# A diffusion trunk in float32: the last FFN's gated units as seven half-size products instead of eight

## The chip, the cores and the metric

The kernel runs on one core of a Trainium2 chip. The metric is the time of the whole program on the device in microseconds (us); the median of three runs is 1763.65 us (1762.95 to 1763.93). Engines are named as the profile names them: PE is TensorE's matmul, PEld its weight load, DVE VectorE, ACT ScalarE, POOL GpSimd, SP SyncE, which issues the loads.

## The reference

Two layers work on 512 latent and 256 context tokens of width 1024: latent attention in layer 0, a state-space layer (S5) with a gated output (GLU) in layer 1, and after each a gated FFN with 2816 hidden units. Each sub-layer begins with an RMSNorm and a modulation (scale and shift computed from a conditioning vector) and ends with a gated residual. Only latent tokens leave layer 1. What the change touches is the second layer's FFN:

```python
def modulate(x, g, shift, scale):
    return rmsnorm(x, g) * (1 + scale) + shift

def swiglu(h, w_in, w_out):
    a, b = jnp.split(h @ w_in, 2, axis=-1)
    return (jax.nn.silu(a) * b) @ w_out

xl = xl + gt2_l * swiglu(modulate(xl, norm_ffn[i], sh2_l, sc2_l), ffn_w_in[i], ffn_w_out[i])
```

## The kernel before

Everything is held transposed: 128 channels on the partitions, tokens along the columns. x has eight such rows of channels (KT = 8). Every float32 product is done as three products of a rounded type: an operand is split into a high part (a copy on ScalarE, rounded) and a low part (the difference, on VectorE; `split`, L74 to L81), and `passes` (L812 to L818) adds high x high, high x low and low x high in PSUM. So a linear layer with eight rows of channels takes 24 matmuls for each 128 outputs, each of them with its own weight load.

The FFN has 22 hidden tiles of 128 units. A *gated unit* is one of them: two weight tiles of 128x1024 (for a and b), two PSUM accumulators of 512 columns, 48 matmuls, then silu(a) on ScalarE (L873), the product with b on VectorE (L874) and the split of the result u. `BLOCKS` (L827) cuts layer 1's 22 units into blocks of 8, 7 and 7. After each block follow eight *output tiles*: the block's u's times `ffn_w_out` (24 or 21 matmuls of 512 columns), added to x on VectorE with the gate (`residual`, L801). After the last block each row of x is stored by SP (L890).

Weights come through one stream (`Stream`, `load`, `halve`, L83 to L125): a specification names the next weight; `take` loads up to two ahead (four, while an extra pool is open) and has one more split ahead. Raw weights, high and low parts have two buffers each (tags w_raw, w_hi, w_lo). `ada_rows` (L243 to L276) computes the rest of the modulation terms on VectorE: for each of eight rows a 128x1024 product with accumulation, two rows a step, pinned to the order of the program (`keep_in_program_order`); in layer 1's FFN they are stepped once a unit. The rest of the order on each engine is chosen by the scheduler when the program is built, which takes, of what it holds ready, the earliest in the program.

Layer 1's FFN comes right behind the GLU, which is done in two halves of 256 tokens (`HALVES`): products of 256 columns, sigmoid, residual, and the sum of squares for the norm. Each half ends with `modulate` (L346 to L356), which makes the FFN's input hh, hl for that half. `first1` computes the first two gated units half by half, so that TensorE works on the first half while the second half's norm is made.

Of the kernel before, what the change touches and what calls it, by code (L numbers as in the profile page):

```python
# [10 lines left out]
F32 = mybir.dt.float32  # L11
F32R = mybir.dt.float32r
AF = mybir.ActivationFunctionType
# [36 lines left out]
def trunk_kernel(ctx: ExitStack, tc: tile.TileContext, ins: dict, outs: dict):  # L50
# [5 lines left out]
    def pool(name, **kw):  # L56
        return tc.tile_pool(name=name, bufs=1, reuse_waits="tile", **kw)
# [242 lines left out]
    def mod(layer, term):  # L300
        return mods[layer][:, 8 * term : 8 * term + 8, :]
# [524 lines left out]

    BLOCKS = ([(0, 5), (5, 10), (10, 14), (14, 18), (18, 22)], [(0, 8), (8, 15), (15, 22)])  # L827

    def ffn_specs(layer):
        for bi, (b0, b1) in enumerate(BLOCKS[layer]):  # L830
            for ht in range(b0, b1):
                for j in range(2):
                    yield ins["ffn_w_in"][layer, ht, j], KT * P, f"wi{layer}_{ht}_{j}", layer * j > 0
            for m in range(KT):
                yield (ins["ffn_w_out"][layer, m, :, b0:b1, :].rearrange("p a b -> p (a b)"), (b1 - b0) * P,
                       f"wo{layer}_{bi}_{m}", layer * m % 2 > 0)

    def specs():
        for p_ in range(2):
            for m in range(KT):  # L840
                yield ins["mla_w_o"][m], KT * P, f"wmo{p_}_{m}", m % 2 == 0 and p_ + m > 0
        yield from ffn_specs(0)
# [5 lines left out]
        yield from ffn_specs(1)  # L848

    stream.specs = iter(specs())  # L850

    def ffn(layer, parts, pf, first, ops, hooks, norm=None, ahead=None):
        blocks = BLOCKS[layer]
        n = parts[-1][2]
        ub = max(b - a for a, b in blocks)
        gate = mod(layer, 5)
        for bi, (b0, b1) in enumerate(blocks):
            uh = pf.tile([P, ub, n], F32R, tag="uh", name=f"uh{layer}_{bi}")
            ul = pf.tile([P, ub, n], F32R, tag="ul", name=f"ul{layer}_{bi}")
            uops = [(part_of(uh, p_), part_of(ul, p_)) for p_ in parts]  # L860
            for ht in range(b0, b1):
                if ht == 0:
                    firsts = first()
                if ht < len(firsts):
                    ab = firsts[ht]
                else:
                    ab = accs_for(parts, f"f{layer}_{ht}", 2)
                    for acc in ab:
                        linear(acc, stream.take(), ops)
                sa = pf.tile([P, n], F32, tag="sa", name=f"sa{layer}_{ht}", bufs=1)  # L870
                u = pf.tile([P, n], F32, tag="u", name=f"u{layer}_{ht}", bufs=1 + layer)
                for acc, accb, (_, a, b) in zip(*ab, parts):
                    nc.scalar.activation(sa[:, a:b], acc, AF.Silu)  # L873
                    nc.vector.tensor_mul(u[:, a:b], accb, sa[:, a:b])  # L874
                split(uh[:, ht - b0, :], ul[:, ht - b0, :], u)
                next(hooks, None)
            for m in range(KT):
                w = stream.take()
                acc, = accs_for(parts, f"fo{layer}_{bi}_{m}")
                linear(acc, w, uops, b1 - b0)  # L880
                for z, p_ in zip(acc, parts):
                    residual(z, p_, m, gate)
                if m in EXTRA:
                    next(hooks, None)
                if norm is not None and b1 == HT:
                    norm.add(m, x[:, m, :])
                    if m == 3:
                        ahead()
                if layer and b1 == HT:
                    nc.sync.dma_start(outs["out"][:, m, :], x[:, m, :NL])  # L890

    def begin(ab, ws, i, ops, ks=range(KT)):

# [4 lines left out]
    with pool("pd") as pd:  # L898
# [48 lines left out]
        with pool("pf0") as pf:  # L947
# [71 lines left out]
            sp, mix = {}, {}  # L1019
            it = hooks0()  # L1020
            norm = Norm(pd, T, "2")
            ffn(0, PARTS, pf, first, ops, it, norm, ahead)
        chunk_roots(norm)


    with pool("pg") as pg:
# [36 lines left out]
        with pool("ph", side="right") as ph, ExitStack() as wx:  # L1063
            more["pool"] = wx.enter_context(pool("wx1"))
            hh = ph.tile([P, KT, NL], F32R, tag="hh", name="hh_f1")
            hl = ph.tile([P, KT, NL], F32R, tag="hl", name="hl_f1")
            tiles = [lambda nm, n: ph.tile([P, n], F32, tag="hm", name=nm, bufs=4)]
            for p_ in HALVES:
                _, a, b = p_
                norm = Norm(ph, b - a, f"3_{a}")  # L1070
                for m in range(KT):
                    if m == 0:
                        ab = [[acc[0][:, a:b]] for acc in both]
                    else:
                        ab = accs_for([p_], f"gl{a}_{m}", 2)
                        for acc in ab:
                            linear(acc, stream.take(), [gated(a, b)])
                    sg = ph.tile([P, b - a], F32, tag="sg", name=f"sg{a}_{m}", bufs=2)
                    nc.scalar.activation(sg, ab[1][0], AF.Sigmoid)
                    z = ph.tile([P, b - a], F32, tag="z", name=f"gz{a}_{m}", bufs=2)  # L1080
                    nc.vector.scalar_tensor_tensor(z, ab[0][0], mod(1, 2)[:, m, 0:1], sg, op0=ALU.mult, op1=ALU.mult)
                    nc.vector.tensor_add(x[:, m, a:b], x[:, m, a:b], z)
                    norm.add(m, x[:, m, a:b])
                modulate(p_, 3, mod(1, 3), part_of(hh, p_), part_of(hl, p_), norm.bcast(), tiles)
# [10 lines left out]
            with pool("pf1") as pf:  # L1095
                ffn(1, [(0, 0, NL)], pf, first1, [(hh, hl)], ada_rows(pf, 40, 48, 2))
    banks.close()


def s5_prep(nc, const, pp, ps1, ins, ident, dsk, i16, sp):  # L1100
# [564 lines left out]
```

## Time and profile before

| | us |
|---|---|
| median of three runs | 1763.65 |
| the profiled execution, own time | 1765.18 |
| its span on the core | 1763.4 |
| busy in it: PE / DVE / ACT / POOL | 1646.2 / 1077.5 / 690.8 / 590.0 |
| last FFN in it, from the end of the GLU (1397) to the end | 366 |

A row of the chain or the timeline begins with the time from the span's start in us and the length in us; "x" is the number of instructions merged in the row. A row of a group gives line, engine, operation, what is written and read, shapes and count, then busy us, the mean of one in ns, and the idle time of the engine just before these instructions with what ended it. A row of the table by stage gives the stretch, its length, the busy us of each engine (with its instructions), TensorE's granted clock as a share of full speed, the busy share of the DMA engines, and GB/s.

### The profile page before, as it was taken

The numbers are of one execution on the slowest core, as the hardware profiler recorded it, in microseconds if no ns is written. First come the engines' busy times: TensorE is split into PE (matmuls) and PEld (weight loads), VectorE is DVE, ScalarE is ACT, GpSimd is POOL, SyncE is SP. The second block draws the span as 40 slices with busy tenths as digits, with TensorE's granted clock in tenths as the row PEclk, the third lists the DMA queues.
The fourth block names the chain that finished last, engine by engine and source line by source line (L and its number), as shares of the span: only waits on it lengthen the run. The fifth ranks groups of instructions, "written<-read, shape, count | busy, mean of one in ns | idle before, by whom it ended". The sixth has DMA issues, their size and how long they took to land. (4 is left out here: it accounts for less than half of the span.)

```text
span 1763.4 us, 29083 instructions
## 1 busy us (share of the span) xinstructions
PE 1646.2 (93%) x11486; PEld 1406.3 (80%) x11486; DVE 1077.5 (61%) x1881; ACT 690.8 (39%) x1400; POOL 590.0 (33%) x626
## 2 busy tenths in 40 slices
PE   6979999999999999999989989976799999999999
PEld 5868878777888887877778878865579988888887
DVE  5787868787997356575566434547965654333332
ACT  3447757677453212222222312246525543232221
POOL 0156454510235247586667300046741100000000
PEclk9999989999999999999999999988879999999999
DMA  9130001124424355566435554353536452333231
GB/s 337 42 119 15 15 12 30 57 81 152 163 85 141 111 176 155 162 195 185 137 117 176 172 203 147 123 180 132 197 123 199 147 175 88 108 91 100 96 88 68
DMA packets 79832, 224.76 MB, mean 127 GB/s; under 512 B 8912, under 2 KB 24144, under 8 KB 77520
## 3 DMA queue, kind: packets, MB, share of 16 engines
q1 hardware_dynamic: 77472, 219.67, 38.4%
q10 hardware_dynamic: 2224, 3.24, 0.5%
q8 instruction: 90, 1.47, 0.3%
q14 instruction: 46, 0.38, 0.1%
HBM read 192.53 MB, written 30.34 MB: 126 GB/s over the span
## 5 line engine op out<-in xcount | busy, mean ns | idle before, releaser
L77 ACT ACTIVATE wh_wi<-wr_wi 128x1024 fp32r<-128x1024 f32 x88 | 93.2, 1061 | 321.6 <-PE f L818 259.5
L80 DVE TENSOR_TENSOR wl_wi<-wr_wi,wh_wi 128x1024 fp32r<-128x1024 f32 x88 | 116.3, 1323 | 130.4 <-ACT wh_wi L77 129.4
L818 PE MATMUL f<-hhh,wl_wi 128*128 128x512 f32 (+1 forms) x704 | 185.5, 341 | 5.0 <-DVE wl_wi L80 5.0
L818 PE MATMUL f<-hhl,wh_wi 128*128 128x512 f32 (+1 forms) x704 | 184.5, 340 | 0.0
L818 PE MATMUL f<-hhh,wh_wi 128*128 128x512 f32 (+1 forms) x704 | 183.7, 340 | 0.1
L818 PE MATMUL fo<-uh,wl_wo 128*128 128x512 f32 (+1 forms) x528 | 161.3, 361 | 9.0 <-DVE wl_wo L80 9.0
L818 PE MATMUL fo<-uh,wh_wo 128*128 128x512 f32 (+1 forms) x528 | 162.7, 364 | 4.3 <-ACT wh_wo L77 2.6
L818 PE MATMUL fo<-ul,wh_wo 128*128 128x512 f32 (+1 forms) x528 | 162.4, 361 | 3.4 <-DVE ul L80 3.4
L326 POOL TENSOR_TENSOR sqa<-sqa,sq 128x256 f32<-128x256 f32 (+2 forms) x25 | 37.9, 1515 | 323.3 <-ACT sq L324 321.5
L77 ACT ACTIVATE wh_wo<-wr_wo 128x512 fp32r<-128x512 f32 (+3 forms) x64 | 50.5, 793 | 239.9 <-PE fo L818 112.7
L818 PE MATMUL f<-hl_f,wh_wi 128*128 128x512 f32 (+1 forms) x384 | 142.8, 372 | 0.0
L818 PE MATMUL f<-hh_f,wl_wi 128*128 128x512 f32 (+1 forms) x384 | 142.6, 372 | 0.0
L818 PE MATMUL f<-hh_f,wh_wi 128*128 128x512 f32 (+1 forms) x384 | 142.1, 372 | 0.0
L801 DVE SCALAR_TENSOR_TENSOR x<-fo,mods,x 128x512 f32<-128x512 f32 x104 | 63.4, 644 | 120.4 <-PE fo L818 120.4
L818 PEld LDWEIGHTS f<-hhh,wl_wi 128*128 128x128 f32 x704 | 109.8, 190 | 21.0 <-DVE wl_wi L80 5.9
L818 PEld LDWEIGHTS f<-hhh,wh_wi 128*128 128x128 f32 x704 | 109.0, 189 | 17.1 <-issue 1.0
L818 PEld LDWEIGHTS f<-hhl,wh_wi 128*128 128x128 f32 x704 | 109.0, 189 | 15.7 <-issue 0.6
L818 PEld LDWEIGHTS fo<-uh,wl_wo 128*128 128x128 f32 x528 | 88.9, 192 | 24.0 <-DVE wl_wo L80 10.0
L818 PEld LDWEIGHTS fo<-uh,wh_wo 128*128 128x128 f32 x528 | 89.3, 193 | 19.7 <-ACT wh_wo L77 3.1
L818 PEld LDWEIGHTS fo<-ul,wh_wo 128*128 128x128 f32 x528 | 89.6, 193 | 18.6 <-DVE ul L80 4.3
L80 DVE TENSOR_TENSOR wl_wo<-wr_wo,wh_wo 128x512 fp32r<-128x512 f32 (+3 forms) x64 | 60.4, 947 | 55.1 <-ACT wh_wo L77 54.9
L709 ACT ACTIVATE pth<-pt 128x384 fp32r<-128x384 f32 (+1 forms) x160 | 71.8, 470 | 42.1 <-PE pt L705 40.7
(401 smaller groups left out, 4033.0 us busy)
## 6 DMA issues: line engine op xcount, KB each, us to landing
wr_wi<-ffn_w_in SPq DMA_DIRECT2D x88, 512.0 KB, 3.7
adaw<-ada_w SPq DMA_DIRECT2D x72, 512.0 KB, 4.5
wr_wg<-s_w_glu SPq DMA_DIRECT2D x30, 512.0 KB, 3.5
adat<-ada_t SPq DMA_DIRECT2D x24, 512.0 KB, 4.9
wr_wmo<-mla_w_o SPq DMA_DIRECT2D x16, 512.0 KB, 3.6
s_wout<-v SPq DMA_DIRECT2D x64, 128.0 KB, 2.6
s_win<-big SPq DMA_DIRECT2D x16, 512.0 KB, 4.8
s5win<-s_win SPq DMA_DIRECT2D x7, 1024.0 KB, 4.8
```

The source lines that it names most:

```text
L77: ins_ = nc.scalar.activation(hi, src, AF.Copy)
L80: eng.tensor_tensor(lo, src, hi.bitcast(F32), ALU.subtract)
L326: nc.gpsimd.tensor_tensor(self.acc, self.acc, sq, ALU.add)
L709: nc.scalar.activation(dh, pt3, AF.Copy)
L801: nc.vector.scalar_tensor_tensor(x[:, m, a:b], acc, gate[:, m, v : v + 1], x[:, m, a:b], op0=ALU.mult, op1=ALU.add)
L818: nc.tensor.matmul(acc, st, xs[lo][:, k, :], start=s, stop=e)
```

## The change

For layer 1 the general `ffn`, its specifications and `first1` go; layer 0 keeps `ffn` unchanged in what it does. Layer 1's first two units (tiles 0 and 1) are still plain products of 256 columns, now ordered by half of the tokens, tile, then half of the channels. The other twenty units use one level of Strassen's algorithm in Winograd's form: the two weight tiles (a over b) are cut into 2 x 2 blocks of 128 x 512, the input into 2 x 2 blocks of four channel rows x 256 tokens; seven products of 4 x 3 matmuls of 256 columns go into four quarters of two PSUM banks, y, z, x and w. Four of their intermediate sums are copied by ScalarE to the tiles r and q, and VectorE puts the rest together.

On the input side the modulated values of each half are kept unsplit (hr), and after the second half's modulation four differences (two on VectorE, two on GpSimd, 128 x 1024 each) and four splits make t1, t2, t3 and the new upper half of the second tokens. On the weight side a class `Ring` loads the raw tiles two units ahead, makes the four combinations on GpSimd (in place, 128 x 512), and splits seven parts into a ring of nine slots. Raw tiles of even units take both w_raw buffers, those of odd units one w_hi and one w_lo buffer; output weights use w_raw, w_hi and w_lo as before. A unit's steps of preparation for the next unit are written between its products.

```diff
-    def ffn(layer, parts, pf, first, ops, hooks, norm=None, ahead=None):
+    def ffn(parts, pf, first, ops, hooks, norm, ahead):
...
-            def first1():
-                abs_ = [accs_for([(0, 0, NL)], f"f1_{i}", 2) for i in range(2)]
-                ws = [[stream.take() for _ in ab] for ab in abs_]
-                for _, a, b in HALVES:
-                    for ab, w in zip(abs_, ws):
-                        begin([[acc[0][:, a:b]] for acc in ab], w, 0, (hh[:, :, a:b], hl[:, :, a:b]))
-                return abs_
...
+                        if a and m == KT - 2:
+                            ring.load(0)
+                            ring.plain(0)
+                        if a and m == KT - 1:
+                            ring.load(1)
...
+                def load_unit(n):
+                    if n < len(units):
+                        bi, ht, _ = units[n]
+                        if ht >= 0:
+                            ring.load(ht)
+                        else:
+                            ahead_[n] = load(*w_out(1, bi, -1 - ht))
...
+                def product(acc, w, b, start):
+                    for k in range(4):
+                        ws = slice(k * P, (k + 1) * P)
+                        for st, mv in ((w[0], b[0]), (w[0], b[1]), (w[1], b[0])):
+                            nc.tensor.matmul(acc, st[:, ws], mv(k), start=start and k == 0 and st is w[0] and mv is b[0],
+                                             stop=(k == 3 and st is w[1]), skip_group_check=True)
...
+                half(0, 0)
+                modulate_half(HALVES[1], norms[1])
+                half(1, 0)
...
+                nc.vector.tensor_sub(h0[:, top], h1[:, top], h0[:, top])
+                nc.gpsimd.tensor_tensor(h1[:, top], h1[:, low], h1[:, top], ALU.subtract)
+                nc.vector.tensor_sub(h1[:, low], h1[:, low], h0[:, top])
+                nc.gpsimd.tensor_tensor(h0[:, low], h0[:, low], h1[:, low], ALU.subtract)
+                half(0, 1)
+                todo = prepare_unit(0)
...
+                for t, raw in ((t1, h0[:, top]), (t2, h1[:, low]), (t3, h1[:, top])):
+                    split(t[0], t[1], raw)
+                    next(todo, None)
+                plain_gate(0)
+                next(todo, None)
+                half(1, 1)
+                load_unit(1)
+                split(hh[:, top, NL // 2 :], hl[:, top, NL // 2 :], h0[:, low])
+                for _ in todo:
+                    pass
+                plain_gate(1)
...
+                WAYS = [(0, b11, "x", True, ("r", 0)), (1, b21, "y", True, None), (2, tq(t1), "z", False, ("q", 1)),
+                        (3, tq(t2), "x", False, ("r", 1)), (4, b22, "z", False, None), (5, tq(t3), "x", False, None),
+                        (6, b12, "w", False, ("q", 0))]
+                for n, (bi, ht, _) in enumerate(units):
+                    b0, b1 = BLOCKS[1][bi]
+                    load_unit(n + 2)
+                    todo = prepare_unit(n + 1)
+                    if ht >= 0:
...
+                        ws = ring.parts.pop(ht)
+                        for i, b, acc, start, to in WAYS:
+                            product(at[acc], ws[i], b, start)
+                            if to:
+                                t = {"r": r, "q": q}[to[0]]
+                                nc.scalar.activation(t[:, 256 * to[1] : 256 * to[1] + 256], at[acc], AF.Copy)
+                            next(todo, None)
+                        nc.vector.tensor_add(r, z[:, 0:512], r)
+                        nc.scalar.activation(r, r, AF.Silu)
+                        two = lambda t: t.rearrange("p (a b) -> p a b", a=2)
+                        nc.vector.tensor_add(two(q), at["x"].unsqueeze(1).to_broadcast([P, 2, 256]), two(q))
+                        nc.vector.tensor_mul(r, r, q)
+                        split(uh[:, ht - b0, :], ul[:, ht - b0, :], r)
+                        next(rows, None)
+                    else:
+                        m = -1 - ht
+                        acc, = accs_for([(0, 0, NL)], f"fo1_{bi}_{m}")
+                        linear(acc, ahead_.pop(n), [(uh, ul)], b1 - b0)
+                        residual(acc[0], (0, 0, NL), m, mod(1, 5))
...
+class Ring:
...
+    SLOTS = 9
...
+    def load(self, ht):
+        tags = ("w_hi", "w_lo") if ht % 2 else ("w_raw", "w_raw")
+        self.raw[ht] = [self.raw_tile(t, f"wr1_{ht}_{j}") for j, t in enumerate(tags)]
...
+    def steps(self, ht):
...
+        done(a11)
+        s1 = self.pool.tile([P, 4 * P], F32, tag="s1", name=f"s1_{ht}")
+        G.tensor_tensor(s1, a21, a22, ALU.add)
+        yield
+        done(a12)
+        G.tensor_tensor(a21, a11, a21, ALU.subtract)
+        G.tensor_tensor(a11, s1, a11, ALU.subtract)
+        yield
+        done(s1)
+        G.tensor_tensor(a12, a12, a11, ALU.subtract)
+        yield
+        for q in (a11, a12, a21, a22):
+            done(q)
+            yield
```

## Rows read from the trace of the kernel before

**Rows 1.** Page, section 1: busy us, share of the span and instructions of TensorE.
```profile
PE 1646.2 (93%) x11486; PEld 1406.3 (80%) x11486; DVE 1077.5 (61%) x1881; ACT 690.8 (39%) x1400; POOL 590.0 (33%) x626
```

**Rows 2.** Chain of waits near its end: start us, length us, engine, line, count.
```profile
1408.28 79.26 PE f L818 x403
1531.05 76.16 PE f L818 x336
```

**Rows 3.** Table by stage: before the second half's modulation, and gated units of block 1.
```profile
1397.00:1408.00 11.00, 11.00 (x95) 11.00 (x94) 2.69 (x6) 1.75 (x3) 0.71 (x1) 1.00 0.31 97
1531.00:1607.00 76.00, 76.00 (x337) 63.00 (x336) 25.27 (x27) 21.09 (x26) 0.00 (x0) 1.00 0.31 91
```

**Rows 4.** Chain of waits in the GLU, whose matmuls have 256 columns.
```profile
1310.84 44.37 PE gl L818 x348
1368.48 28.80 PE gl L818 x240
```

**Rows 5.** Groups by shape, from 1408 us to the end.
```profile
L77 ACT ACTIVATE wh_wi<-wr_wi 128x1024 fp32r<-128x1024 f32 x40 | 42.2, 1060 | 126.0 <-PE f L818 93.6 <-PE fo L818 32.3
L80 DVE TENSOR_TENSOR wl_wi<-wr_wi,wh_wi 128x1024 fp32r<-128x1024 f32 x40 | 48.9, 1226 | 88.1 <-ACT wh_wi L77 87.2
L80 DVE TENSOR_TENSOR wl_wo<-wr_wo,wh_wo 128x896 fp32r<-128x896 f32 x16 | 17.3, 1091 | 26.8 <-ACT wh_wo L77 26.7
L80 DVE TENSOR_TENSOR ul<-u,uh 128x512 fp32r<-128x512 f32 x22 | 15.2, 692 | 14.7 <-ACT uh L77 14.7
L874 DVE TENSOR_TENSOR u<-f,sa 128x512 f32<-128x512 f32 x22 | 15.1, 684 | 0.5 <-ACT sa L873 0.5
L77 ACT ACTIVATE wh_wo<-wr_wo 128x896 fp32r<-128x896 f32 x16 | 15.0, 952 | 51.8 <-PE f L818 25.8 <-PE fo L818 18.8 <-issue 7.2
L77 ACT ACTIVATE uh<-u 128x512 fp32r<-128x512 f32 x22 | 13.9, 632 | 29.3 <-DVE u L874 29.3
L873 ACT ACTIVATE sa<-f 128x512 f32<-128x512 f32 x22 | 12.8, 581 | 0.0
```

**Rows 6.** Timeline of VectorE and GpSimd in two stretches of layer 0's FFN.
```profile
858.93 1.02 DVE L874 TENSOR_TENSOR u<-f,sa 128x512 f32<-128x512 f32 x2 [3.65 <-PE f L818]
859.87 2.11 DVE L80 TENSOR_TENSOR wl_wi<-wr_wi,wh_wi 128x1024 fp32r<-128x1024 f32 x1
858.14 1.37 POOL L1266 TENSOR_TENSOR ot<-bc,apr 128x512 f32<-128x512 f32 x1
859.59 1.30 POOL L1267 TENSOR_TENSOR v<-ot,ot 128x512 f32<-128x512 f32 x1
860.98 2.01 POOL L1262 TENSOR_TENSOR ot<-gr,hr 128x384 f32<-128x384 f32 x1
832.10 1.99 DVE L80 TENSOR_TENSOR wl_wi<-wr_wi,wh_wi 128x1024 fp32r<-128x1024 f32 x1 [3.35 <-ACT wh_wi L77]
833.09 2.15 POOL L1267 TENSOR_TENSOR v<-ot,ot 128x512 f32<-128x512 f32 x1
835.32 1.14 POOL L1262 TENSOR_TENSOR ot<-gr,hr 128x384 f32<-128x384 f32 x1
```

**Rows 7.** Groups by shape of GpSimd: its one operation of 1024 columns.
```profile
L80 POOL TENSOR_TENSOR w0l<-wr_wg,w0h 128x1024 fp32r<-128x1024 f32 x2 | 4.8, 2400 | 2.3 <-ACT w0h L77 2.2
```

**Rows 8.** Groups by shape of VectorE, 510 to 1135 us (layer 0's FFN).
```profile
L80 DVE TENSOR_TENSOR wl_wi<-wr_wi,wh_wi 128x1024 fp32r<-128x1024 f32 x44 | 62.5, 1421 | 37.3 <-ACT wh_wi L77 37.3
```

**Rows 9.** Timeline of VectorE: the end of the second half's modulation; back-to-back operations.
```profile
1415.01 0.76 DVE L80 TENSOR_TENSOR hl_f<-hm,hh_f 128x256 fp32r<-128x256 f32 x2 [1.15 <-ACT hh_f L77]
1426.44 0.69 DVE L80 TENSOR_TENSOR ul<-u,uh 128x512 fp32r<-128x512 f32 x1
1427.04 0.69 DVE L874 TENSOR_TENSOR u<-f,sa 128x512 f32<-128x512 f32 x1
```

**Rows 10.** Groups by shape of ScalarE: a read of 256 columns from PSUM.
```profile
L1079 ACT ACTIVATE sg<-gl 128x256 f32<-128x256 f32 x16 | 5.8, 368 | 2.1 <-PE gl L818 2.1
```

**Rows 11.** Page, section 6: loads, KB each, median us to landing.
```profile
wr_wi<-ffn_w_in SPq DMA_DIRECT2D x88, 512.0 KB, 3.7
```

More of the change, by code (lines that the diff above doesn't have):

```diff
@@ L884, in ffn @@
                     next(hooks, None)
-                if norm is not None and b1 == HT:
+                if b1 == HT:
                     norm.add(m, x[:, m, :])
@@ L1021, in trunk_kernel @@
             norm = Norm(pd, T, "2")
-            ffn(0, PARTS, pf, first, ops, it, norm, ahead)
+            ffn(PARTS, pf, first, ops, it, norm, ahead)
         chunk_roots(norm)
@@ L1062, in trunk_kernel @@
         right.close()
-        with pool("ph", side="right") as ph, ExitStack() as wx:
-            more["pool"] = wx.enter_context(pool("wx1"))
+        with pool("ph", side="right") as ph, pool("pw") as pw:
             hh = ph.tile([P, KT, NL], F32R, tag="hh", name="hh_f1")
             hl = ph.tile([P, KT, NL], F32R, tag="hl", name="hl_f1")
[L1067 to L1073, printed above, removed]
-                    else:
[L1075 to L1084, printed above, removed]
-            def first1():
-                abs_ = [accs_for([(0, 0, NL)], f"f1_{i}", 2) for i in range(2)]
-                ws = [[stream.take() for _ in ab] for ab in abs_]
-                for _, a, b in HALVES:
-                    for ab, w in zip(abs_, ws):
-                        begin([[acc[0][:, a:b]] for acc in ab], w, 0, (hh[:, :, a:b], hl[:, :, a:b]))
-                return abs_
-            with pool("pf1") as pf:
-                ffn(1, [(0, 0, NL)], pf, first1, [(hh, hl)], ada_rows(pf, 40, 48, 2))
@@ L1097, in trunk_kernel, with modulate_half @@
-    banks.close()
+            hr = [ph.tile([P, KT, NL // 2], F32, tag="hr", name="hr0")]
+            ring = Ring(nc, pw, split, raw_tile, lambda ht, j: ins["ffn_w_in"][1, ht, j])
+            norms = [Norm(ph, NL // 2, f"3_{a}") for _, a, _ in HALVES]
+            def modulate_half(p_, norm):
+                tiles = [lambda nm, n, k=k: hr[-1][:, k, :] for k in range(KT)]
+                modulate(p_, 3, mod(1, 3), part_of(hh, p_), part_of(hl, p_), norm.bcast(), tiles)
+            with pool("wx1") as wx:
+                more["pool"] = wx
+                for p_, norm in zip(HALVES, norms):
+                    _, a, b = p_
+                    for m in range(KT):
+                        if m == 0:
+                            ab = [[acc[0][:, a:b]] for acc in both]
+                        else:
+                            ab = accs_for([p_], f"gl{a}_{m}", 2)
+                            for acc in ab:
+                                linear(acc, stream.take(), [gated(a, b)])
+                        if a and m == KT - 2:
[3 more added lines that the diff above has]
+                            ring.load(1)
+                        sg = ph.tile([P, b - a], F32, tag="sg", name=f"sg{a}_{m}", bufs=2)
+                        nc.scalar.activation(sg, ab[1][0], AF.Sigmoid)
+                        z = ph.tile([P, b - a], F32, tag="z", name=f"gz{a}_{m}", bufs=2)
+                        nc.vector.scalar_tensor_tensor(z, ab[0][0], mod(1, 2)[:, m, 0:1], sg, op0=ALU.mult, op1=ALU.mult)
+                        nc.vector.tensor_add(x[:, m, a:b], x[:, m, a:b], z)
+                        norm.add(m, x[:, m, a:b])
+                    if a == 0:
+                        modulate_half(p_, norm)
+                more["pool"] = None
@@ new lines, in trunk_kernel, with __init__, slot, quarters @@
+    banks.close()
+class Ring:
+    SLOTS = 9
+    def __init__(self, nc, pool, split, raw_tile, src):
+        self.nc, self.pool, self.split, self.raw_tile, self.src = nc, pool, split, raw_tile, src
+        self.raw, self.parts, self.n = {}, {}, 0
+    def load(self, ht):
+        tags = ("w_hi", "w_lo") if ht % 2 else ("w_raw", "w_raw")
+        self.raw[ht] = [self.raw_tile(t, f"wr1_{ht}_{j}") for j, t in enumerate(tags)]
+        for j in range(2):
+            self.nc.sync.dma_start(self.raw[ht][j], self.src(ht, j))
+    def slot(self):
+        self.n += 1
+        return [self.pool.tile([P, 4 * P], F32R, tag=f"ring{c}", name=f"w{c}1_{self.n}", bufs=self.SLOTS) for c in "hl"]
+    def quarters(self, ht):
+        return [w[:, 512 * k : 512 * k + 512] for w in self.raw.pop(ht) for k in range(2)]
+    def plain(self, ht):
+        self.parts[ht] = []
+        for q in self.quarters(ht):
+            hi, lo = self.slot()
+            self.split(hi, lo, q)
+            self.parts[ht].append((hi, lo))
+    def steps(self, ht):
+        a11, a12, a21, a22 = self.quarters(ht)
+        out = self.parts[ht] = []
+        G = self.nc.gpsimd
+        def done(q):
+            out.append(self.slot())
+            self.split(*out[-1], q)
+        done(a11)
[11 more added lines that the diff above has]
+            done(q)
+            yield
```

86 lines of the change are left out of this document (71 added, 15 removed).

## The prediction

> **What bounds the kernel now.** I read the page first, for TensorE's share of the span [rows 1], then the chain of waits from its end backwards. The six rows before its last, from 1408 to 1760 us, are all TensorE without a gap: gated units and output tiles in turn, block by block, of which block 0's and block 1's gated units stand here [rows 2]. The last FFN is worth what its matmuls cost. 336 of 512 columns took 76.16 us, 226.7 ns from one start to the next. The table by stage shows the clock at 1.00 (the 2.4 GHz level) with TensorE busy all of the time, while VectorE has 25.3 and ScalarE 21.1 of 76 us, and GpSimd nothing [rows 3]. The groups show why these cost nothing today: ScalarE's weight copies sat idle 93.6 us waiting for a buffer that TensorE held [rows 5]. The other engines follow TensorE; the question is whether they still can when each has more to do.
>
> **The products.** Twenty units (hidden tiles 2 to 21) go from 48 matmuls of 512 columns to 7 x 4 x 3 = 84 of 256. The price of a 256-column matmul stands in the GLU, in the same order of operands: 240 in 28.80 us, 120 ns [rows 4]. So a unit goes from 48 x 226.7 = 10.88 us to 84 x 120 = 10.08: -0.80, and **-16.0 us** over twenty. An eighth fewer columns gives 7.4% of the time, because every matmul carries some 13 ns beside its columns (2 x 120 - 226.7 = 13.3) and there are 75% more of them. The other GLU stretch, 348 in 44.37 us or 127.5 ns, is the bound on the other side: -3.4 us. I take 120, the row that stands nearest to the FFN and has no start of a stage in it. Each of those 240 matmuls had a weight load of its own, so a pace set by loads is in that price. The first two units keep 192 matmuls of 256 columns as before.
>
> **What VectorE and GpSimd get.** A unit prepared two 128x1024 low parts; now it prepares seven of 128x512 (seven weight combinations), with four additions on GpSimd, two PSUM additions, one product and the low part of u on VectorE: eleven operations of some 0.69 us [rows 5] instead of two of 1.23 and two of 0.69. Alone that is 7.6 of 10.08 us. But the two engines disturb one another. At 859.59 GpSimd starts a 128x512 operation, VectorE a 128x1024 subtraction at 859.87; the latter takes 2.11 us, ending 1.09 us after GpSimd's end, and the next GpSimd operation takes 2.01 us, though the same one took 1.14 at 835.32, ending 1.01 after VectorE's. At 833.09 a 128x512 one ends 1.15 us after VectorE's [rows 6]. They take turns: 1.09 us for 1024 columns on VectorE (0.545 for 512), 1.15 for 512 on GpSimd, some 2.3 for 1024 [rows 7]. VectorE's two products from PSUM at 858.93 took their usual 1.02 us beside GpSimd's at 858.14 [rows 5, 6], so operations with a PSUM operand need no turn. The Trainium skill says so too (SBUF — State Buffer, "Who interferes with whom"): a VectorE instruction with two SBUF inputs and a GpSimd one that reads SBUF block each other fully, whoever starts first. By that rule the sum is the one below. The mean over the first FFN speaks more mildly: 1.42 us there [rows 8] instead of 1.23 without GpSimd [rows 5], a factor 1.16, by which a unit needs 8.8 of 10.08 us and nothing is lost (first rival). I go by turns, as the single rows show them.
>
> A settled unit then needs nine turns of 0.545 and four of 1.15: 9.5 us of 10.08. It fits, by 0.6 us. The ring frees part i when product i is done, so a part is due some 8 us after it may be made; short delays cost nothing.
>
> **Block 0** has more to do. The second token half is modulated until 1415.8 [rows 9]. From there to the first output tile stand: two differences and four splits of 1024 columns on VectorE (6 x 1.09 = 6.5), two differences on GpSimd (4.6), the parts of six units (6 x 8.4 = 50.5, less 4.0 for one part and three GpSimd additions that can run earlier), eight gates (7.6), the eight adaLN rows that stay pinned in these units (8.7), one output weight (1.1): 75.0 us, ending at 1490.8. TensorE alone would end at 1487.5 - 4.8 = 1482.7. Before, the stage ended at 1487.5 [rows 2]. So block 0 is bound by the turns and comes to **+3.3 us** instead of -4.8. Lower bound -4.8 (no turns), upper +12.9 (third rival). That modulation now feeds products which take the upper and lower half of the rows apart costs nothing on top, TensorE having time to spare there.
>
> **Blocks 1 and 2**: seven settled units, 66.5 us of turns and 1.0 for an output weight, under 70.6 of TensorE: **-5.6 each, -11.2**.
>
> **Ends of blocks.** After the last product: copy (0.37, as the GLU's sigmoid from PSUM [rows 10]), add, product, split: 0.37 + 0.68 + 0.69 + 0.63 + 0.69 = 3.1 us [rows 5] until the last u exists. The output tile needs it after 7 x 3 x 0.227 = 4.8 us in block 0, 4.1 in the others. Cover is 1.0 us; a weight copy and subtraction ahead of it would cost 1.3. I take 0.3 each, **+1.0** (0 to 3.8).
>
> **Loads.** Unit n+2 is loaded at the start of unit n, with the same 512 KB pieces landing in 3.7 us [rows 11] and due 10 us later: hidden. Behind a waiting load in SP's queue stand only later loads and the output rows. One place has no cover: raw weights of odd tiles take the buffers of the split weights. At output tile 6 of block 1, tile 15's load takes the free one, so tile 7's split waits until TensorE is through with tile 6: 0.95 (copy) + 1.09 (subtraction) [rows 5] less two matmuls, **+1.6** (0 if the scheduler gives the buffer to the split).
>
> **PSUM copies.** Counted from 0, product 4 adds to what product 2 left in PSUM and product 5 to what product 3 left, so ScalarE must have copied each within the product between: 1.44 us of cover for 0.37 us of work. One part copy ahead (0.63 [rows 5]) still fits, two miss by some 0.2; at two places in twenty units that would be 8 us. ScalarE has 7 x 0.63 + 4 x 0.37 + 0.58 + 0.63 = 7.1 of 10.08 us, so 0. The eight splits of 512 instead of four of 1024 in the GLU lie in idle time.
>
> **Sum:** 3.3 - 11.2 + 1.0 + 1.6 = -5.3 us. The profiled execution took 1765.2 us (1.8 outside its span), 1.5 above the median of the runs, so 1759.9 there is 1758.4 in terms of the median.
>
> **The rivals.** *No drag in block 0:* VectorE is busy 2.7 of 11 us from 1397 to 1408 [rows 3]; if enough is put there, or turns cost only the mean factor, block 0 gives its -4.8 and the sum is -13.4: 1750.3. Against it: most of the parts wait for ring slots that TensorE frees later. 0.25.
> *Block 0 eats it all:* if the pinned rows stand ahead of the next unit's parts, a unit costs 12.3 us while they last (9.5, 2.2 for two rows, 0.6 of hand-offs), four times 2.2 over TensorE's 10.1; and of the 11.1 us of differences and splits some 6.4 fit beside the first two units (1415.8 to 1422.2), so the third starts 4.7 late. Block 0 ends at 1482.7 + 8.9 + 4.7 = 1496.3, +8.8; the sum is +0.2, 1763.8. For it: nothing lets the rows wait. 0.18.
> *VectorE becomes the bound (slower):* if the two PSUM additions never fall beside a GpSimd turn, VectorE's cycle is 11 x 0.60 (start to start, [rows 9]) + 4 x 1.15 = 11.2 us, more than the 10.88 of before, which is the point from which it decides. Block 0 then takes 75.0 + 16 x 0.6 = 84.6 us, +12.9; the others 7 x 11.2 + 1.0 less 4.8 prepared during the last output tile, 74.6, -1.6 each; with +2.6 for ends and the split: +12.3, 1776. For it: VectorE works strictly in order; against: GpSimd's additions can run ahead whenever a raw weight is there. 0.17.
>
> **How the numbers follow.** My case has 0.40 and its own range 1754 to 1763. Some 0.2% (3.5 us) is what a measurement of this kernel can tell from no change. Faster: 0.25 + 0.32; same: 0.08 + 0.13; slower: 0.05 + 0.17. The range 1750 to 1770 leaves out the third rival and a little below the first.
>
> **What would show it.** Right: 120 ns from start to start in a unit; f stretches of 70.6 us in blocks 1 and 2; in block 0 an f stretch that ends near 1490, with TensorE idle on the low parts of the ring or of t1 to t3; subtractions of 512 columns that last up to 1.7 us beside GpSimd. Wrong: TensorE idle on ScalarE's PSUM copies in every unit, units over 10.9 us in block 2, a pace off 120 ns, or an f stretch of 60 us after the first two units.

## The result, and the profile after

The changed kernel takes 1822.39 us (median of 4 runs, 1819.95 to 1827.33) against 1763.34 for the kernel before in the same series: **ratio 1.0331, 95% interval 1.0307 to 1.0354. It is slower by 59 us**; 1758.4 was forecast, with a range to 1770. The profiled execution took 1819.95 us. Its page (span; busy us, share of the span, instructions):

```profile
span 1818.2 us, 31131 instructions
PE 1656.7 (91%) x12206; PEld 1445.6 (80%) x12206; DVE 1208.5 (66%) x2031; ACT 759.5 (42%) x1586; POOL 725.4 (40%) x708
```

The chain of waits, start us, length us, engine, line, count, from block 1's units to the output tiles of block 1, and a piece of what follows. Before, this was TensorE alone [rows 2].

```profile
1562.09 24.57 PE f L1133 x190
1587.05 1.79 DVE r L1221
1588.88 0.51 issue
1589.39 0.61 ACT wh L77
1590.33 19.00 PE f L1133 x156
1609.72 1.79 DVE r L1221
1612.07 0.61 ACT wh L77
...
1636.91 4.79 PE fo L818 x21
1641.70 1.44 PE f L1133 x12
1643.60 4.58 PE f L1133 x36
1648.62 0.70 DVE r L1217
1649.34 0.64 ACT r L1218
1650.01 0.70 DVE r L1221
1650.74 0.64 ACT uh L77
1651.42 23.38 PE fo L818 x90
1674.80 3.71 DMA wr<-ffn_w_in
```

Two things are to be seen. The price of the products is as forecast: 12 in 1.44 us, 120 ns. But TensorE no longer runs through: VectorE's product of the gate (L1221, 1.79 us instead of 0.69), a weight copy of ScalarE behind it, and at the end of the block the whole gate, from add to split, stand in the chain.

TensorE's waits from 1397 us to the end, of which the kernel before has none (who waits, for whom: us in total, times, longest):

```profile
PE f L1133 <- ACT q L1215: 12.1, 6, 2.3
PE f L1133 <- ACT r L1215: 11.4, 8, 4.3
PE fo L818 <- ACT uh L77: 9.8, 3, 3.3
PE f L1133 <- DVE hl_f L80: 3.8, 3, 2.3
PE f L1133 <- ACT wh L77: 2.9, 1, 2.9
PE f L1133 <- DVE r L1180: 2.4, 1, 2.4
PE f L1133 <- DVE wl L80: 1.7, 1, 1.7
PE fo L818 <- ACT wh_wo L77: 0.8, 1, 0.8
```

The table by stage of the same execution answers to [rows 3] (length; busy us and count of TensorE, weight loads, VectorE, ScalarE, GpSimd; then the granted clock):

```profile
1408.00:1440.00 32.00, 21.56 (x136) 20.02 (x135) 30.68 (x32) 18.64 (x35) 19.86 (x11) 0.77 0.11 33
1562.00:1651.00 89.00, 81.10 (x610) 78.77 (x610) 61.87 (x73) 42.52 (x84) 35.07 (x23) 0.96 0.23 69
1651.40:1653.00 1.60, 1.58 (x4) 1.25 (x5) 0.69 (x1) 0.00 (x0) 0.00 (x0) 0.50 0.00 0
1653.00:1655.00 2.00, 2.00 (x6) 1.07 (x5) 1.47 (x2) 1.80 (x2) 0.00 (x0) 0.50 0.00 0
1657.00:1659.00 2.00, 2.00 (x10) 1.60 (x9) 0.00 (x0) 0.00 (x0) 0.00 (x0) 0.89 0.85 233
```

The largest two rows of the waits, 23.5 of 44.9 us, are ScalarE's copies out of PSUM (L1215), which the forecast had at nothing. The last three rows of the table show a second cost: after the 3.25 us of idle before the first output tile of block 1, the granted clock is 0.50 (the 1.2 GHz level), and 6 matmuls stand in 2 us where 10 do once it has risen (last row, 0.89).

**The books close.** From the end of the GLU's last matmuls (1368.48 + 28.80 = 1397.28 before [rows 4], 1396.22 after) to the end of the span the kernel before takes 1763.4 - 1397.28 = 366.1 us, the changed one 1818.2 - 1396.22 = 422.0. Adding up over all matmuls there: the products at 120 and 226.7 ns give the -16.0 of the forecast; idle gaps give 44.8; and 27 are start-to-start times longer than those prices, some 22 of it in matmuls at the lower clock (ten stretches of 3 to 10 us at 0.50), the rest mostly what each wait costs beside its length (some 0.27 us, see the end). 366.1 - 16.0 + 44.8 + 27 = 421.9. So the gain was made in full, and 72 us were added to it. I use this stage (called **the FFN stage** below) to compare kernels, because the part ahead of it varies from build to build and run to run: in the changed kernel and its variants below, with the same code up to there, the GLU ends between 1391.4 and 1404.7.

### The profile page after: what moved, and what is told of

It is laid out like the page before. It is cut to its first block, busy times and chain, and to the rows that moved or that the text cites. A ratio compares the mean times of both kernels' runs of the same rounds, so it can differ in the third digit from the quotient of the medians.

```text
span 1818.2 us, 31131 instructions
## 1 busy us (share of the span) xinstructions
PE 1656.7 (91%) x12206; PEld 1445.6 (80%) x12206; DVE 1208.5 (66%) x2031; ACT 759.5 (42%) x1586; POOL 725.4 (40%) x708
## 5 line engine op out<-in xcount | busy, mean ns | idle before, releaser
L818 PE MATMUL fo<-uh,wh_wo 128*128 128x512 f32 (+1 forms) x528 | 166.7, 372 | 14.9 <-ACT uh L77 11.4
L818 PE MATMUL fo<-ul,wh_wo 128*128 128x512 f32 (+1 forms) x528 | 166.7, 369 | 2.9 <-DVE ul L80 2.9
L80 DVE TENSOR_TENSOR wl<-wr,wh 128x512 fp32r<-128x512 f32 x128 | 119.1, 947 | 33.4 <-ACT wh L77 32.4
L1133 PE MATMUL f<-hh_f,wh 128*128 128x256 f32 x384 | 113.1, 296 | 16.6 <-ACT r L1215 11.4
L77 ACT ACTIVATE wh_wi<-wr_wi 128x1024 fp32r<-128x1024 f32 x44 | 46.7, 1061 | 188.0 <-PE f L818 165.4
L1133 PE MATMUL f<-hl_f,wh 128*128 128x256 f32 x384 | 112.8, 294 | 3.8 <-DVE hl_f L80 3.8
L1133 PE MATMUL f<-hh_f,wl 128*128 128x256 f32 x384 | 112.4, 293 | 1.7 <-DVE wl L80 1.7
L77 ACT ACTIVATE wh<-wr 128x512 fp32r<-128x512 f32 x128 | 78.6, 627 | 83.5 <-PE f L1133 49.3
L1133 PE MATMUL f<-t,wh 128*128 128x256 f32 x480 | 93.1, 292 | 12.1 <-ACT q L1215 12.1
```

The lines of the kernel that those rows point to most:

```text
L77: ins_ = nc.scalar.activation(hi, src, AF.Copy)
L80: eng.tensor_tensor(lo, src, hi.bitcast(F32), ALU.subtract)
L818: nc.tensor.matmul(acc, st, xs[lo][:, k, :], start=s, stop=e)
L1133: nc.tensor.matmul(acc, st[:, ws], mv(k), start=start and k == 0 and st is w[0] and mv is b[0], stop=(k == 3 and st is w[1]), skip_group_c ...
```

## The experiments

Two theories at first. **T**: VectorE and GpSimd take turns, so VectorE is late, ScalarE stands in order behind it, and TensorE waits for ScalarE's copies. **R**: the order that the build gives TensorE (output tiles ahead of a block's last products, products without cover) makes the waits. All results together, FFN stage worked out as above (e3, i1, i2 and some others: from the last GLU matmul, since products stand between them):

```
                          us      FFN stage  TensorE idle  longer starts
before                  1763.34     366.1        0.0            0
after                   1822.39     422.0       44.8           27
e1 no GpSimd additions  1793.33     396.1       30.7           15
e2 output tiles last    1814.94     417.7       39.1           28
e3 additions on VectorE 1797.36     397.2       32.4           15
e4 early add            1826.71     429.3       52.5           27
g1 e3, written order    1832.23     438.2       64.3           24
g2 g1, more cover       1853.11     452.9       75.7           27
g3 g2 with GpSimd       1867.38     469.5       86.5           33
g4 g2, start on VectorE 1853.02     452.9       75.8           27
h1 two PSUM tiles       1789.67     387.1       23.1           14
h2 h1 + e3              1760.79     367.6        9.7            8
h3 h2, written order    1774.35     367.9       11.0            7
h4 h2, output tiles last 1768.52    367.5       10.2            7
i2 h2, start's order    1766.14     364.9        8.3            7
i1 i2, late splits      1769.17     366.8        9.3            7
j1 i2, third plain unit 1763.05     364.6        7.4            6
j2 h2, third plain unit 1758.50     364.6        6.8            6
```

(One run each but j1, and the stage is read from one trace each; the kernel before took 1761.51, 1764.54, 1766.08, 1764.83 and 1767.94 beside e, g, h, i and j. Its 13 runs beside j lay between 1755.53 and 1774.89, so one total alone tells little. "Longer starts" are counted above the 1.5 us that the kernel before has too.)

**e1**, which leaves the four GpSimd additions of each unit out and splits raw quarters instead:

```diff
-        G.tensor_tensor(s1, a21, a22, ALU.add)
-        G.tensor_tensor(a21, a11, a21, ALU.subtract)
-        G.tensor_tensor(a11, s1, a11, ALU.subtract)
-        G.tensor_tensor(a12, a12, a11, ALU.subtract)
```

> Leaves out the four GpSimd additions of each of the twenty units; raw weight quarters are split in their place, so VectorE, ScalarE, TensorE and the loads do the same work and only GpSimd's is gone. Theory T (VectorE and GpSimd take turns at their SBUF operands, VectorE falls behind, ScalarE waits in order for it, TensorE idles and falls to half clock): 512-column subtractions come down from a mean of 0.96 to about 0.70 us, TensorE's idle after 1397 us falls from 45 to at most 20 us and the time to 1785 us or less. Theory R (TensorE's order at block ends, which the scheduler fixed at build time, and the buffers shared by units and output tiles make most of the idle): subtractions come down too, but the time stays at 1800 us or more.

Measured: the stage is 25.9 us shorter; between both thresholds. Two of VectorE's groups in the changed kernel (count | busy us, mean ns of one | idle before):

```profile
L80 DVE TENSOR_TENSOR wl<-wr,wh 128x512 fp32r<-128x512 f32 x124 | 116.4, 955 | 32.7 <-ACT wh L77 31.8
L1221 DVE TENSOR_TENSOR r<-r,q 128x512 f32<-128x512 f32 x20 | 19.2, 958 | 1.0 <-ACT r L1218 0.5
```

The same groups in e1:

```profile
L80 DVE TENSOR_TENSOR wl<-wr,wh 128x512 fp32r<-128x512 f32 x144 | 97.1, 687 | 63.8 <-ACT wh L77 61.9 <-PE f L1133 1.5
L1221 DVE TENSOR_TENSOR r<-r,q 128x512 f32<-128x512 f32 x20 | 13.7, 686 | 1.1 <-ACT r L1218 0.6
```

The turns are real. But 30.7 us of idle stay without them.

**e3**, the same additions on VectorE (`G = self.nc.vector`):

> The four additions go from GpSimd to VectorE, which then has 15 operations of about 0.60 us, 9.0 us, in a unit of 10.08, and nobody to take turns with. Theory T: no wait of VectorE for GpSimd is left, 512-column subtractions take 0.69 us; VectorE alone nearly fills a unit, so some idle stays: 1780 to 1800 us. Theory R: within 8 us of the changed kernel, 1812 to 1828. If more work on VectorE is what hurts, whoever does the rest: slower, over 1828.

It held: 1797, and 24.8 us off the stage. But eleven waits of exactly 0.88 us for one of ScalarE's copies remained in the units, with no GpSimd operation near and VectorE's subtractions at their 0.68 us. T does not explain these.

**e2** and **e4** test R at the ends of blocks:

```diff
-                        linear(acc, ahead_.pop(n), [(uh, ul)], b1 - b0)
+                        with tc.issue_after(end.ins):
+                            linear(acc, ahead_.pop(n), [(uh, ul)], b1 - b0)
```

> Output tiles may stand on TensorE only behind the last product of their block (an ordering edge, no new wait). Before, the first two output tiles were mixed in ahead of the last unit's products, and each block's remainder then waited 3.25 us for the last u, with half clock after it. Theory R: these three waits shrink to below 1 us and the time falls by 12 to 20 us, to 1802-1810. Theory T: the waits inside the units stay, and the time falls by less than 6 us because the products that now come earlier wait for their parts.

e4 moves the gate's add and Silu (L1217, L1218) behind the fifth product:

> The addition into r and its silu are written behind product 4, when their inputs are complete, instead of behind product 6, so the chain behind the last product of a block loses two steps (0.68 and part of 0.63 us). Theory R: the three waits of 3.25 us before the output tiles fall to about 2.5, and the time by 2 to 5 us. Theory T: the same there, and the 2.2 us waits inside blocks 1 and 2, where ScalarE's split of u stands behind VectorE's late product, stay: within 5 us of the changed kernel.

e2: the three waits of 3.25 us become 0.36 us or nothing, yet the stage gains only 4.3, since the last products, no longer spread between output tiles, wait for copies instead. e4: the waits before the output tiles fall to 2.6 us or less, but those inside the units grow to 3.3, and the stage is 7.3 us longer, where theory R had the time fall (the total is 4.3 us above the changed kernel's median, inside T's 5). So R, read as an order at the ends of blocks, is a small part.

**g1 and g2** went after the 0.88 us: TensorE held to the written order of products (g1), then another order with two products between a result and the product that overwrites it (g2).

```diff
+                            with tc.issue_after(end.ins) if end else ExitStack():
+                                end = product(at[acc], ws[i], b, start)
```

> The four additions on VectorE as in e3, and TensorE held to the order in which the products are written: each product behind the last matmul of the one before, output tiles behind the last product. Theory H (the waits of 0.88 us that e3 still shows in each unit come from the build-time order, which puts the product that overwrites a quarter of PSUM right behind the one whose result ScalarE has to copy out of it): in the order as written one product of 12 x 0.12 = 1.44 us lies between, the copy and its hand-overs take about 0.9 us, so the waits within units go except where a part's split (0.63 us) stands ahead of the copy; idle falls from 32 to 15-22 us with the three waits of 3.25 us, the time to 1775-1787. Theory V (VectorE at 15 operations of 0.61 us in a unit of 10.08 us is what keeps the pace, and TensorE's waits are only where that surfaces): the waits move and stay, 1793-1800.

> As g1, and the seven products in another order (1, 3, 2, 4, 7, 5, 6 of the written ones, the parts of the weights made in that order too), so that two products of 1.44 us lie between a result and the product that overwrites it, and the last copy of a unit comes two products before its end. Theory H: no wait on a copy within a unit is left, even with a split ahead of the copy (0.63 + 0.37 + hand-overs under 2.88 us); what is left is the start (7 us of idle) and the changes to and from the output tiles; idle 8-14 us, 1763-1775. Theory V: VectorE's operations are as many as in g1 and e3, so the time stays within 5 us of g1's and not below 1785.

Both were far off: the stage is 41 and 56 us longer than e3's. This was the most useful result. More cover made more waits. The first two of TensorE's waits in g1, by whom they wait for:

```profile
PE f L1133 <- ACT r L1218: 42.7, 39, 7.3
PE f L1133 <- ACT q L1218: 16.0, 20, 1.4
```

The timeline of g1 at one of them (start, length, engine, line, and in brackets the idle time before and what ended it):

```profile
1575.03 0.28 PE L1133 MATMUL f<-t,wl 128*128 128x256 f32 x1
1575.23 0.63 ACT L77 ACTIVATE wh<-wr 128x512 fp32r<-128x512 f32 x1 [0.29 <-PE f L1133]
1575.77 0.37 ACT L1218 ACTIVATE q<-f 128x256 f32<-128x256 f32 x1
1576.18 0.50 PE L1133 MATMUL f<-t,wh 128*128 128x256 f32 x2 [0.88 <-ACT q L1218]
```

59 waits in twenty units: three in each but one, one behind every copy that has a product after it in the unit (in g2, where all four have one, 79). Here the third product has written quarter z; its copy runs until 1576.14; the fourth, which writes quarter x in the other bank, starts 0.04 us later. The built program says why: in each unit of g1 the second product, into columns 0 to 255, carries a wait for the copy that reads columns 512 to 767. The kernel makes the four quarters in one PSUM tile of 1024 columns (`z = ps2(...)`), and whatever is written into that tile after a read of any part of it waits for that read. In g1 each of the three products writes the other bank than the one that the copy reads: y behind the copy of x, x behind that of z, z behind that of x. The build's own order had hidden much of this by putting products of the next unit between.

**g3 and g4** ask what the turns cost in this setting, and whether the start can be eased by VectorE:

> As g2 but with the four additions on GpSimd, as in the changed kernel. Theory T (VectorE and GpSimd take turns, and the turns cost by themselves): VectorE's subtractions stay at up to 1.8 us, its product of the gate comes late, ScalarE stands in order behind it, and even two products of cover are not always enough: 1785-1805, some 15-30 us above g2. Theory H alone: within 8 us of g2, because a late copy has 2.88 us to come.

> As g2, with the two subtractions of 2048 columns that GpSimd makes at the start of the FFN on VectorE too (2 x 2.1 to 2.3 us there, for 2.8 and 7.5 us on GpSimd in e3). If GpSimd's turns at the start are what delays the split of the second half there (one VectorE instruction of 0.4 us took 2.58 us beside it), the waits of 2.3 and 3.2 us at the start shrink and the time falls by 2-4 us against g2; if VectorE's own queue is full there, it stays within 1 us or rises by up to 3.

g3's stage is 16.6 us longer than g2's: the turns cost here as T expects. That two products of cover did not take the waits away, in g2 already, shows that there was no such cover. g4 gains nothing: the waits at the start only move.

**h1 to h4**: theory **B**, the shared tile. The quarters get two tiles of one bank:

```diff
-                        z = ps2(f"f1_{ht}")
-                        at = {"y": z[:, 0:256], "z": z[:, 256:512], "x": z[:, 512:768], "w": z[:, 768:1024]}
+                        z, xw = ps1(f"f1_{ht}"), ps1(f"f1x_{ht}")
+                        at = {"y": z[:, 0:256], "z": z[:, 256:512], "x": xw[:, 0:256], "w": xw[:, 256:512]}
```

(with `use_banks("psum_f", 1, 8)` ahead of the loop, and output tiles from `ps1` too).

> Theory B, formed from g1 and g2 (a wait of 0.88 us right behind each of ScalarE's copies, three in each unit of g1 and four in g2, whatever quarter the next product writes; in the built program of g1 the second product, which writes the first bank, carries a wait for the copy out of the second bank): the four quarters are one PSUM tile of two banks, and every product behind a copy waits for that copy. Here the quarters are two tiles of one bank each, eight such tiles in turn, and GpSimd keeps its additions. B: the waits of 0.88 us go, and a late copy has a product of 1.44 us to come; the turns (e1, e3: 21 to 27 us) stay in part: 1785-1805. Theory T alone: the copies are late because VectorE is, and the tile changes little: 1815-1825.

> As h1, with the four additions on VectorE (e3). B and T together: no wait on a copy within a unit, no turns; what is left is the start (7 us of idle, 4.7 half clock in e3), the three waits of 3.25 us or less before output tiles, and the late split of an output tile: 1765-1780. Were VectorE's load (15 operations of 0.61 us in a unit of 10.08) the bound instead, the units would stay at the 11.2 us of e3 and the time at 1790-1797.

> As h2, with TensorE held to the written order of products and output tiles (as g1, which without the change of tiles took 1832). B: with no false wait the written order has a product of cover behind each copy, and the output tile's first 21 matmuls (4.8 us) cover the end of the block: 3-8 us below h2, 1760-1775. If it was the order itself that cost in g1, it stays above h2 by 20 us or more.

> As h2, with the output tiles alone held behind the last product (as e2), products left to the build-time order: the waits of 3.25 us go; 3-8 us below h2, within 4 us of h3 on either side.

h1, the change of tiles alone, takes 34.9 us off the stage; with the additions on VectorE as well (h2) 54.4, and 1760.79, below the range expected, is the first time at the level of the kernel before (1766.08 beside it). What h1 still waits for copies, and its row of the table by stage that stands beside the changed kernel's from 1562 to 1651 us:

```profile
PE f1x L1133 <- ACT r L1216: 9.2, 5, 5.9
PE f L1133 <- ACT q L1216: 5.2, 8, 1.0
```

```profile
1562.00:1651.00 89.00, 85.77 (x605) 79.43 (x604) 65.94 (x76) 41.71 (x82) 30.46 (x20) 1.00 0.24 75
```

The waits for copies are 14.4 us instead of 23.5, with 5.9 of it in one wait at the start. The three waits for the last u (9.8 us on `uh`) are gone, and of the ten stretches at 0.50 two are left. So the 34.9 us are not the waits inside the units alone: h1 also gives each output tile one of eight single banks, instead of one of three tiles of two banks, and its build puts only 12 to 15 matmuls of output tiles ahead of a block's last products. What this part is worth was not tried apart. The false wait's own price is clearest between g1 and h3, which have the same written order and no wait for the last u: 59 waits for copies with 58.7 us become three with 5.5, and the stage falls by 70.3 us.

h3 and h4 have the stage of h2 within 0.3 us, not 3 to 8 us less as expected: the waits at the ends of blocks were already gone in h2. Once the false wait is gone, TensorE's order is worth nothing; g1's +41 was the false wait, which the written order leaves uncovered. (Their totals are higher by what stands ahead of the GLU's end.) TensorE's waits in h2 from the end of the GLU on (some 0.4 us in smaller ones left out):

```profile
PE f1x L1133 <- ACT r L1216: 3.0, 1, 3.0
PE f L1133 <- POOL hl_f L80: 2.6, 1, 2.6
PE fo L818 <- ACT wh_wo L77: 2.2, 5, 0.8
PE f L1133 <- DVE hl_f L80: 1.2, 2, 0.7
PE fo L818 <- ACT uh L77: 0.3, 1, 0.3
```

The table by stage for 35 us of h2's block 1:

```profile
1555.00:1590.00 35.00, 35.00 (x294) 35.00 (x293) 32.72 (x55) 22.84 (x47) 0.00 (x0) 1.00 0.17 57
```

No wait is left in a settled unit: TensorE has 35.00 of 35 us, at a clock of 1.00. VectorE stands at 32.72, 93%, and still follows. The Trainium skill (Perfetto Trace Analysis, "Matmuls" under "Optimizing Tensor Performance") asks for independent groups of matmuls to go through different PSUM banks, so that emptying one overlaps filling the next. The kernel did that by columns, and g1 shows that columns don't suffice here; h2, where each bank is a tile, shows the overlap.

**i2, i1: the start.** h2's stage is still 1.5 us longer than before's, because 6.7 us of idle stand between 1404 and 1430. i2 puts all splits of the second half on VectorE, and the four differences behind them; i1 also issues the plain units' gate splits later.

```diff
+                with tc.issue_after(last.ins):
+                    nc.vector.tensor_sub(h0[:, top], h1[:, top], h0[:, top])
```

> h2 with another order at the start of the FFN: all splits of the second half, and the four subtractions for the tiles of the Strassen products, on VectorE, the subtractions behind the last of those splits. In h2 TensorE waits there 0.71, 0.49, 2.56 us for splits of the second half that stand behind a 1024-column pass on VectorE and GpSimd, and then 2.96 us for the copy of the first Strassen unit. If the order makes the first three, they shrink to under 1.5 us together, 2-4 us are won from the end of the GLU to the end of the kernel (367.8 us in h2: 364-366). If VectorE is simply full there (some 30 operations between 1402 and 1428), the wait only moves behind to the copy, 366-369.

> As i2, and the splits of the plain units' gates issued behind products 1 and 5 of the first Strassen unit, so that ScalarE's copy out of PSUM there does not stand behind them. If it is these splits that the copy stands behind (2.96 us in h2), that wait goes as well: from the end of the GLU to the end of the kernel 360-364 us, below the 364.5 of the kernel before for the first time. If not, it stays within 1 us of i2.

(The 364.5 quoted there for the kernel before is too low; its stage is 366.1.) i2: the first three waits shrink from 3.76 to 0.71 us as expected, but the wait for the first copy grows from 2.96 to 4.49; the stage falls by 2.7. i1 missed: that wait is 5.47, so the gate's splits are not its cause. From 1411 to 1438 VectorE in i2 is busy 25.16 of 27 us.

**j1, j2** test VectorE's load there by giving it time: a third unit of plain products ahead of the first Strassen unit.

```diff
-                units = units[2:]
+                units = units[3:]
```

(its parts from `ring.plain(2)`, its two halves ahead of the splits of t1 to t3 and of b12).

> i2 with a third unit of plain products (48 x 0.227 = 10.9 us for 84 x 0.12 = 10.1: 0.8 us more of products) ahead of the first Strassen unit, so that VectorE has 10.9 us more for the tiles that the Strassen products read. Theory: at the start VectorE is full (in i2 without a gap from 1410 to 1438), and the 4.5 us of TensorE idle before the first t product, with its half clock after, is that queue. Then the wait goes: from the end of the GLU to the end of the kernel 359-362 us (365.2 in i2, 366.4 before), and the ratio to before is 0.995-0.999. If the wait is a dependency rather than VectorE's load, it moves by a unit and the time stays at 365-367.

> As j1 without i2's order: the third split of each three in the second half and two of the four subtractions stay on GpSimd, as in h2. The splits of the second half wait beside GpSimd as in h2 (3.8 us in all), the first Strassen unit does not: 1.5-4 us above j1.

j1's wait before the t products is gone, but another of 4.46 us stands at 1432, now for the gate of a plain unit (L1183, on VectorE). So the wait did not go with the products that read t1 to t3; that it follows VectorE's queue fits this, but is not shown (VectorE in i2 is 93% busy there, not "without a gap"). The stage, 364.6, did not reach the 359 to 362 expected. j2, expected 1.5 to 4 us above j1, has the same 364.6. How to relieve the start stays open. Over three rounds **j1's ratio to before is 0.9986, interval 0.9959 to 1.0013: no difference** that can be told. No version beat the kernel before measurably.

## Why the prediction was wrong

- **Products: right.** 12 in 1.44 us and, in h2, 24 in 2.88: 120 ns; all 16.0 us are there (14.6 in j1 and j2, which have one Strassen unit less).
- **PSUM copies "so 0": the step that failed.** It took the two hazards that the arithmetic has (product 4 after the copy of 2's quarter, 5 after 3's) for all that would be waited for, and 8 us for the upper bound. The unit of waiting is the PSUM tile, not the quarter: every product behind a copy waits for it. In the changed kernel 23.5 of 44.8 us of idle are waits for such copies, false and true ones together, with the lower clock behind several of them; two tiles in place of one take 34.9 of the 55.9 us away (h1, the ends of blocks included). In h1 14.4 us of these waits stay, in h2, without the turns, 3.0: a copy that comes late costs also with the tiles apart. The listed sign for "wrong" (TensorE idle on ScalarE's PSUM copies) is the one that appeared, though not in every unit: 14 waits in twenty units.
- **Turns: the size of one right, the conclusion half right.** Subtractions of 512 columns beside GpSimd last up to 1.8 us, near the 1.7 foretold, and the turns do fit into the time (VectorE busy 61.87 of 89 us). But "short delays cost nothing" was false in the changed kernel (e3: 24.8 us), because ScalarE, in order behind a late VectorE, delivered the copy late, and the tile left TensorE no other product to go on with. With the quarters in two tiles it comes nearer: in h1, with all turns in place, TensorE is busy 85.77 of 89 us from 1562 to 1651, against 81.10 in the changed kernel. Still, GpSimd's additions cost 19.5 us there (h1 against h2): 7.1 up to the last output tile of block 0, 12.4 after it.
- **Block 0: the direction right, the size not.** It was called bound by the turns and put at +3.3. From the GLU's end to the last output tile of block 0 the kernel before takes 133.8 us, the changed one 161.7: 27.9 more. There the changed kernel loses some 32 us to idle and longer starts, h1 some 20, h2 some 13: also without GpSimd's additions VectorE is nearly full at the start (i2).
- **Ends of blocks (+1.0): wrong.** The cover was worked out for the written order. The build put all matmuls of the first two output tiles that don't need the last u (2 x 18, the 15 and 21 around the last products in the chain) ahead of the unit's end, and none was left as cover: three waits of 3.25 us, with 3 to 6 us at the lower clock behind each. In h2, where output tiles have banks of their own, the build leaves enough of them as cover, and 0.3 us of such waits is left (1.4 more for weight copies there), within the term's bounds.
- **Late split of an output tile (+1.6)**: 0.8 after, 0.81 in h2; in e1 one such wait was 4.5. The right kind. **Loads "hidden": not quite.** At both changes from output tiles to units a load of the next unit stands in the chain (1674.80, 3.71 us), as its buffer came free late; after the first, TensorE waited 2.9 us for a weight copy (the row of `ACT wh`).
- **The clock had no term.** TensorE busy without a gap had it at 1.00; every idle time was counted at its length. Of the 27 us of longer starts some 22 are matmuls at 0.50.
- **Rivals.** "VectorE becomes the bound" had the sign, not the mechanism: VectorE was busy 61.87 of 89 us in the table above, far from full. No rival had TensorE and ScalarE handing one tile back and forth.

## What to carry to other kernels

Before a buffer is shared by parts (quarters of a PSUM tile, halves of a ring slot), find out at what grain the framework orders reads and writes, and give each part that must overlap a tile of its own; a wait for another engine's copy behind every product, whatever it writes, is the sign. When work moves from the engine that is the bound to others, count each place where that engine now waits for an answer, and price an idle time with the slower clock that can follow it. Here the products saved their 16 us in nearly every variant, and with the false waits and the turns gone the kernel came out even with the one before: what is left of idle and longer starts, some 13 to 18 us, eats the gain.

## What was not expected of the hardware

- Not each idle time costs the clock. In g1 three waits of some 0.88 us in every settled unit left it at 1.00; after 3.25 us (1648 to 1651) it was 0.50 until 1657. Of two like waits in the changed kernel the first (2.24 us, 1588 to 1590) left it at 1.00 and the second (2.26 us, 1610 to 1613) was followed by 0.50 until 1616. What decides between these was not tried.
- A wait of 0.88 us costs some 1.15: a unit of g1 takes 13.5 us where 10.08 and three waits make 12.7. Part of it is the first matmul after the wait (0.23 us to the next, in place of 0.12); for the rest, the last one before the wait lasts to its end (0.28 us) instead of giving way to the next after 0.12.
